# 18 instead of 20 k-tiles' adaLN on TensorE, and queries and gates of four heads moved forward, in a hybrid attention layer

## Chip, core and metric

The kernel runs on one core of a Trainium2 chip. The metric is the device time of one execution in microseconds (us), here the median of three runs. Engines are named as in the profile: TensorE (PE, with its weight loads PEld), VectorE (DVE), ScalarE (ACT), GpSimd (POOL) and SyncE (SP), whose queue issues most transfers.

## What is computed

One layer with 256 latent tokens and 256 context tokens of width 4096, all in float32. `mod` is the adaLN: a vector times a 4096 x 12288 matrix, once for `c` and (two thirds of it) once for `c_ctx`.

```python
mod = silu(c) @ ada_w + ada_b                    # shift, scale, gate: 4096 each
mod_c = silu(c_ctx) @ ada_w[:, :2*D] + ada_b[:2*D]
h  = rms_norm(x, norm_w)   * (1 + scale)   + shift
hc = rms_norm(ctx, norm_w) * (1 + scale_c) + shift_c
proj = h @ w_in                                  # queries, keys, values, gates of both groups
pc   = hc @ w_ctx                                # keys and values of the context
...                                              # A: 8 heads of differential attention; B: 8 heads of retention
y = concat([o_d * silu(dg), o_r * silu(rg)]) @ w_out
out = x + gate * y
```

## The kernel before

**Tiling.** The 4096 input features are 32 k-tiles of 128. `hs[kt]` holds k-tile kt of `h` and `hc`, transposed, for all 512 tokens, as a hi and a lo part; it exists only when the k-tile's shift and scale are known and `modulate` (L274) has applied them. Every weight tile is loaded in float32 and split too: ACT casts the hi part (L386), VectorE subtracts for the lo part (L387), and three matmuls (hi·hi, hi·lo, lo·hi) make a product (L400 to L402). A *unit* is two k-tiles of one head. A key/value unit ("kv") multiplies four row tiles (latent and context), 24 matmuls of 512 columns for a head of group A and of 384 for group B. A query/gate unit ("qg") needs the latent tokens alone: two row tiles, 12 matmuls. `run_units` (L435) prepares the weights of the next unit (`prep`, L373: three raw buffers, four hi and four lo buffers of one k-tile each), runs a unit and calls a function between units, which appends other work.

**Opening part** (to about 492 us). The first `K1` = 20 k-tiles have their adaLN on TensorE: `Ada.unit` (L240) multiplies eight k-tiles of `ada_w` by a padded `c` (matmuls `pa`, L254), and `finish` (L262) brings a chunk of two output k-tiles to the partitions with short matmuls against `sel` (L270). Between these run the kv units of heads A0 to A5 for the k-tiles that are ready (`SUnit`, L523); the sums of A0 to A4 lie in SBUF and VectorE adds to them (L559).

**First parts** (492 to 954 us). The heads in `FIRST` (A6, A7, B0 to B7) run their kv units over the first 20 k-tiles. Each head's partial sums are copied by ACT and stored to DRAM (`store_part`, L589). Meanwhile VectorE computes the adaLN of the other 12 k-tiles, in chunks of four: `ada2_task` (L296) is a generator; one step takes a slice of `ada_w` (two transfers of 256 KB) and does two accumulations (L318, L320), one for `c` and one for `c_ctx`. After 32 slices TensorE sums the accumulators over the partitions, one column at a time (L328), and `modulate` makes four more `hs`. `between1` (L607) deals the 99 steps out evenly over the first 90 of 100 units.

**Rest** (954 to about 2172 us), in the order of `SCHED`: per head, "kv" over the last 12 k-tiles, whose stored part is loaded four units before the end (L484) and added by VectorE (L495); then "qg" over all 32 k-tiles. Attention or retention of the head before runs in steps between the units (`between`, L969), and so does the gate's share of the adaLN (`gate_task`, L910), two steps a unit in "kv" of group A, one in group B, none in "qg". **Output projection**: from about 2172 us to the end.

The tile framework makes the instruction order of each engine from the order of the program and its own timing estimate, so an instruction whose inputs are ready can move ahead of its place in the program. The right-hand pool `a4` has 41 slots, which `hs`, the heads' tiles and the accumulators share.

Of the kernel before, what the change touches and what calls it, by code (L numbers as in the profile page):

```python
# [20 lines left out]
KT = D // P  # L21
# [17 lines left out]
K1 = 20  # L39
CHUNKS = [1, 1] + [2] * 9  # L40
CHUNKS2 = [4, 4, 4]
# [41 lines left out]
def hybrid_kernel(es, tc, x, c, ctx, c_ctx, norm_w, ada_w, ada_b, w_in, q_norm_w, k_norm_w,  # L83
# [21 lines left out]
    for k in "AB":  # L105
        for h in range(8):
            for i in range(2):
                p_dram[f"{k}{h}", i] = dram.tile([P, 2, 512 if k == "A" else 384], F32, name=f"p_dram{k}{h}_{i}")
# [187 lines left out]
    def ada2_task():  # L296

        work = [(j, k) for j in range(len(CHUNKS2)) for k in range(KT)]
        ahead = []

        def load():
            if len(ahead) < len(work):
                j, k = work[len(ahead)]
                ahead.append(ada_load(c0s2[j], CHUNKS2[j], k, f"ada2_{j}_{k}")[0])

# [3 lines left out]
        for i, (j, k) in enumerate(work):  # L309
            w = ahead[i]  # L310
            cn = CHUNKS2[j]
            n = cn * P
            if k == 0:
                acc = [a4.tile([P, 2 * n], F32, name=f"acc{j}_{v}", tag="a4") for v in range(2)]
            for v in range(2):
                cv = cT[:, v, k:k + 1]
                if k == 0:
                    nc.vector.tensor_scalar(acc[v], w, cv, None, op0=ALU.mult)  # L318
                else:
                    nc.vector.scalar_tensor_tensor(acc[v], w, cv, acc[v], op0=ALU.mult, op1=ALU.add)  # L320
            load()
            if k == KT - 1:
# [154 lines left out]
    def head_units(hd, qg, ktseq, part=False, rest=False):  # L477
# [6 lines left out]
        def before():  # L484
            for i in range(2):
                hd.dst(2 * i, 0)
                nc.sync.dma_start(hd.t[i], p_dram[hd.name, i])

        def after():
# [8 lines left out]
            if part:  # L498
                store_part(hd)
# [89 lines left out]
    def store_part(hd):  # L589

        for i in range(2):
            nc.scalar.dma_start(p_dram[hd.name, i], hd.t[i])
            hd.t[i] = None
# [9 lines left out]
    n_units = len(FIRST) * K1 // 2  # L603
    n_steps = len(CHUNKS2) * (KT + 1)
    done = [0, 0]

    def between1(i):  # L607
        done[0] += 1
        while done[1] < n_steps and done[1] < done[0] / (n_units - 10) * n_steps:
            next(ada2, None)  # L610
            done[1] += 1

    for nm in FIRST:
        run_units(head_units(heads[nm], 0, pairs(0, K1), part=True), between1)
# [363 lines left out]
    for item in SCHED:  # L978
# [9 lines left out]
        if kind == "qg":  # L988
            run_units(head_units(hd, 1, pairs(0, KT)), between)
# [100 lines left out]
```

## Time and profile before

| what | value |
|---|---|
| median of 3 runs | 2545.53 us (2541.44 to 2547.76) |
| the profiled execution | 2544.53 us, span of its instructions 2542.7 us |
| mean granted TensorE clock | 0.991 |
| busy: TensorE, its weight loads, VectorE, ACT | 99%, 84%, 68%, 39% |
| moved over the span | 563.70 MB, mean 222 GB/s |

Busy shares are averages over parts with different limits. The busy time of TensorE is modelled, so the pitch at which its units follow each other says more. The granted clock is the share of 2.4 GHz that TensorE was given; 0.50 is 1.2 GHz.

### The profile page before, as it was taken

What the parts mean: (1) busy time and instruction counts of PE and PEld (TensorE: products, weight loads), DVE (VectorE), ACT (ScalarE), POOL (GpSimd) and SP (SyncE); (2) the same over time, 40 slices, a digit from 0 to 9 for tenths busy, and PEclk for the clock granted to TensorE, in tenths of its full rate; (3) what the DMA queues carried; (4) which work ended last, traced back from release to release, by engine and by line L of the source; (5) the groups of instructions that cost most, each with busy time, mean ns of one, the idle gap of its engine ahead of it and who ended that gap; (6) DMA issues with size and microseconds to landing.
All of it is one profiled execution on the core that took longest, in us unless ns stands there. A gap on an engine that the chain in (4) does not pass through costs nothing.

```text
span 2542.7 us, 36389 instructions
## 1 busy us (share of the span) xinstructions
PE 2508.3 (99%) x12634; PEld 2123.9 (84%) x12634; DVE 1726.4 (68%) x3026; ACT 992.2 (39%) x2017; POOL 44.6 (2%) x47
## 2 busy tenths in 40 slices
PE   7999999999999999999999999999999999999999
PEld 4566666888999997788888788899999999878887
DVE  5555555795897946777876887777777666655554
ACT  4222222222323233354445444554444444544443
POOL 0000000000000000000000000000000000000000
PEclk8999999999999999999999999999999999999999
DMA  9987978785686748766776676556666556676765
GB/s 315 291 284 243 292 230 292 244 269 176 198 274 192 252 105 278 235 219 196 239 241 202 201 238 227 185 178 199 198 207 203 169 152 189 197 238 207 229 208 175
DMA packets 497240, 563.70 MB, mean 222 GB/s; under 512 B 31696, under 2 KB 385296, under 8 KB 497056
## 3 DMA queue, kind: packets, MB, share of 16 engines
q1 hardware_dynamic: 480336, 526.57, 65.7%
q10 hardware_dynamic: 16720, 34.81, 4.0%
q8 instruction: 99, 1.62, 0.3%
q14 instruction: 85, 0.70, 0.1%
HBM read 538.17 MB, written 23.09 MB: 221 GB/s over the span
## 4 chain that ended last, share of the span: by engine, by line
PE 91%; DMA 5%; DVE 2%; SPq 1%; issue 1%; ACT 0%; DVEq 0%; ACTq 0%
PE psA L401 7%; PE psA L402 7%; PE psA L400 7%; PE psB L401 6%; PE psB L402 6%; PE psB L400 6%; PE psO L400 5%; PE psO L401 5%; PE psO L402 5%; PE pa L254 3%; DMA graw<-in_ada_w_dram 2%; DMA ada<-in_ada_w_dram 1%; DMA ostg<-o_dram 1%; SPq L219 1%; PE psA2s L551 1%; PE psA3s L551 1%
## 5 line engine op out<-in xcount | busy, mean ns | idle before, releaser
L386 ACT CAST whiB<-rawB 128x384 fp32r<-128x384 f32 x512 | 258.8, 512 | 455.5 <-PE psB L402 176.9
L387 DVE TENSOR_TENSOR wloB<-rawB,whiB 128x384 fp32r<-128x384 f32 x512 | 279.4, 553 | 170.7 <-ACT whiB L386 166.5
L386 ACT CAST whiA<-rawA 128x512 fp32r<-128x512 f32 x392 | 241.2, 620 | 380.9 <-PE psA L402 251.5
L401 PE MATMUL psA<-wloA,h 128*128 128x512 f32 x896 | 357.8, 399 | 2.6 <-DVE wloA L387 2.5
L402 PE MATMUL psA<-whiA,h 128*128 128x512 f32 x896 | 355.5, 397 | 0.0
L387 DVE TENSOR_TENSOR wloA<-rawA,whiA 128x512 fp32r<-128x512 f32 x392 | 268.3, 687 | 113.2 <-ACT whiA L386 112.3
L400 PE MATMUL psA<-whiA,h 128*128 128x512 f32 x896 | 319.2, 398 | 0.2 <-ACT whiA L386 0.2
L401 PE MATMUL psB<-wloB,h 128*128 128x384 f32 x896 | 303.4, 339 | 1.4 <-DVE wloB L387 1.3
L402 PE MATMUL psB<-whiB,h 128*128 128x384 f32 x896 | 301.7, 337 | 0.0
L387 DVE TENSOR_TENSOR wloO<-rawO,whiO 128x512 fp32r<-128x512 f32 x256 | 175.1, 691 | 154.9 <-ACT whiO L386 154.4
L400 PE MATMUL psB<-whiB,h 128*128 128x384 f32 x896 | 263.4, 339 | 1.9 <-ACT whiB L386 1.8
L386 ACT CAST whiO<-rawO 128x512 fp32r<-128x512 f32 x256 | 157.1, 620 | 198.1 <-PE psO L402 161.5
L320 DVE SCALAR_TENSOR_TENSOR acc<-ada,cT,acc 128x1024 f32<-128x1024 f32 x186 | 233.7, 1277 | 0.0
L934 DVE SCALAR_TENSOR_TENSOR gacc<-graw,cT,gacc 128x512 f32<-128x512 f32 x248 | 184.8, 745 | 49.1 <-DMA graw<-in_ada_w_dram 47.1
L401 PEld LDWEIGHTS psA<-wloA,h 128*128 128x128 f32 x896 | 168.7, 188 | 43.6 <-DVE wloA L387 5.1
L401 PE MATMUL psO<-wloO,o 128*128 128x512 f32 x512 | 203.2, 397 | 0.0
L402 PE MATMUL psO<-whiO,o 128*128 128x512 f32 x512 | 202.8, 396 | 0.0
L400 PEld LDWEIGHTS psA<-whiA,h 128*128 128x128 f32 x896 | 168.5, 189 | 40.0 <-ACT whiA L386 0.5
L402 PEld LDWEIGHTS psA<-whiA,h 128*128 128x128 f32 x896 | 168.7, 188 | 38.9
L401 PEld LDWEIGHTS psB<-wloB,h 128*128 128x128 f32 x896 | 168.5, 188 | 4.1 <-DVE wloB L387 3.6
L402 PEld LDWEIGHTS psB<-whiB,h 128*128 128x128 f32 x896 | 168.5, 188 | 0.3
L400 PEld LDWEIGHTS psB<-whiB,h 128*128 128x128 f32 x896 | 163.0, 188 | 3.9 <-ACT whiB L386 3.2
(395 smaller groups left out, 4250.4 us busy)
## 6 DMA issues: line engine op xcount, KB each, us to landing
ada<-in_ada_w_dram SPq DMA_DIRECT2D x512, 256.0 KB, 4.7
rawA<-in_w_in_dram SPq DMA_DIRECT2D x392, 256.0 KB, 3.4
rawB<-in_w_in_dram SPq DMA_DIRECT2D x256, 256.0 KB, 3.1
graw<-in_ada_w_dram SPq DMA_DIRECT2D x128, 512.0 KB, 5.0
rawO<-in_w_out_dram SPq DMA_DIRECT2D x128, 512.0 KB, 4.5
rawB<-in_w_in_dram SPq DMA_DIRECT2D x256, 128.0 KB, 2.8
p_dramA<-kvqgA ACTq DMA_DIRECT2D x16, 512.0 KB, 2.8
kvqgA<-p_dramA SPq DMA_DIRECT2D x16, 512.0 KB, 6.7
```

What stands on the lines that cost most here:

```text
L219: nc.sync.dma_start(t[:, :, s], ada_w[k0 * P:(k0 + m) * P, s * D + c0 * P:s * D + c0 * P + n] .rearrange("(k p) n -> p k n", p=P))
L254: m = nc.tensor.matmul(self.pa[32 * g:32 * (g + 1), :], cpad[:, 2 * kt:2 * kt + 32], tiles[k], start=(u0 == 0 and i < 4), stop=(u0 + nk == ...
L320: nc.vector.scalar_tensor_tensor(acc[v], w, cv, acc[v], op0=ALU.mult, op1=ALU.add)
L386: nc.scalar.copy(hi, raw[:, k])
L387: nc.vector.tensor_tensor(lo, raw[:, k], hi.bitcast(F32), op=ALU.subtract)
L400: nc.tensor.matmul(pt[:, :ncol], a, hi, start=f, stop=False)
L401: nc.tensor.matmul(pt[:, :ncol], a, lo, start=False, stop=False)
L402: nc.tensor.matmul(pt[:, :ncol], b, hi, start=False, stop=e)
L551: nc.tensor.matmul(pt, a, hi, start=f, stop=False)
L934: nc.vector.scalar_tensor_tensor(acc, raw[:, k], cT[:, 0, kt:kt + 1], acc, op0=ALU.mult, op1=ALU.add)
```

## The change

`K1` becomes 18: the opening part has ten chunks instead of eleven (two single k-tiles, then pairs), and VectorE gets 14 k-tiles, a chunk of two and three of four. A step for the chunk of two takes two k-slices of 256 columns each for shift and scale (four accumulations of 512 columns). The qg units of A0 to A3 over the first 18 k-tiles join the first parts, after B7: their part is stored, and their "qg" in the rest covers 14 k-tiles and adds the part (`NQ` = 4). `between1` no longer counts units: each unit has a weight (`room`: 4.2 us for a kv unit of A, 3.0 for one of B, 1.4 for a qg unit), and the 116 steps are dealt out in proportion, to be through at 0.96 of the total.

```diff
--- before.py
+++ after.py
@@ -36,9 +36,11 @@
 
 
 
-K1 = 20
-CHUNKS = [1, 1] + [2] * 9
-CHUNKS2 = [4, 4, 4]
+K1 = 18
+CHUNKS = [1, 1] + [2] * 8
+CHUNKS2 = [2, 4, 4, 4]
+
+NQ = 4
 LEAD = 0.3
 NS = 6
 ADAB = 6
@@ -104,7 +106,7 @@
     p_dram = {}
     for k in "AB":
         for h in range(8):
-            for i in range(2):
+            for i in range(3):
                 p_dram[f"{k}{h}", i] = dram.tile([P, 2, 512 if k == "A" else 384], F32, name=f"p_dram{k}{h}_{i}")
 
     def aux_tile(shape, name):
@@ -295,31 +297,31 @@
 
     def ada2_task():
 
-        work = [(j, k) for j in range(len(CHUNKS2)) for k in range(KT)]
+        work = [(j, k) for j, cn in enumerate(CHUNKS2) for k in range(0, KT, 4 // cn)]
         ahead = []
 
         def load():
             if len(ahead) < len(work):
                 j, k = work[len(ahead)]
-                ahead.append(ada_load(c0s2[j], CHUNKS2[j], k, f"ada2_{j}_{k}")[0])
+                ahead.append(ada_load(c0s2[j], CHUNKS2[j], k, f"ada2_{j}_{k}"))
 
         for _ in range(ADAB - 1):
             load()
         yield
-        for i, (j, k) in enumerate(work):
-            w = ahead[i]
+        for i, (j, k0) in enumerate(work):
             cn = CHUNKS2[j]
             n = cn * P
-            if k == 0:
+            if k0 == 0:
                 acc = [a4.tile([P, 2 * n], F32, name=f"acc{j}_{v}", tag="a4") for v in range(2)]
-            for v in range(2):
-                cv = cT[:, v, k:k + 1]
-                if k == 0:
-                    nc.vector.tensor_scalar(acc[v], w, cv, None, op0=ALU.mult)
-                else:
-                    nc.vector.scalar_tensor_tensor(acc[v], w, cv, acc[v], op0=ALU.mult, op1=ALU.add)
+            for q, w in enumerate(ahead[i]):
+                for v in range(2):
+                    cv = cT[:, v, k0 + q:k0 + q + 1]
+                    if k0 + q == 0:
+                        nc.vector.tensor_scalar(acc[v], w, cv, None, op0=ALU.mult)
+                    else:
+                        nc.vector.scalar_tensor_tensor(acc[v], w, cv, acc[v], op0=ALU.mult, op1=ALU.add)
             load()
-            if k == KT - 1:
+            if k0 + 4 // cn == KT:
                 yield
                 pm = aux_tile([P, cn, 4], f"pm2_{j}")
                 for q in range(cn):
@@ -482,8 +484,8 @@
         bank = Bank(f"ps{hd.name}{'p' if part else ''}_{qg}", nrt)
 
         def before():
-            for i in range(2):
-                hd.dst(2 * i, 0)
+            for i in (2,) if qg else (0, 1):
+                hd.dst(2 * i, qg)
                 nc.sync.dma_start(hd.t[i], p_dram[hd.name, i])
 
         def after():
@@ -496,7 +498,7 @@
                 else:
                     evict(d, bank.t[rt][:, :hd.ncol])
             if part:
-                store_part(hd)
+                store_part(hd, qg)
 
         for i, (kt0, nk) in enumerate(ktseq):
             last = i == len(ktseq) - 1
@@ -586,9 +588,9 @@
     for h in range(HB):
         heads[f"B{h}"] = Head("B", h)
 
-    def store_part(hd):
-
-        for i in range(2):
+    def store_part(hd, qg=0):
+
+        for i in (2,) if qg else (0, 1):
             nc.scalar.dma_start(p_dram[hd.name, i], hd.t[i])
             hd.t[i] = None
 
@@ -600,18 +602,24 @@
 
     ada2 = ada2_task()
     next(ada2)
-    n_units = len(FIRST) * K1 // 2
-    n_steps = len(CHUNKS2) * (KT + 1)
-    done = [0, 0]
-
-    def between1(i):
-        done[0] += 1
-        while done[1] < n_steps and done[1] < done[0] / (n_units - 10) * n_steps:
+    firsts = [(nm, 0) for nm in FIRST] + [(f"A{h}", 1) for h in range(NQ)]
+    n_steps = sum(KT * cn // 4 + 1 for cn in CHUNKS2)
+
+
+    def room(nm, qg):
+        return (1.4 if qg else 4.2) if nm[0] == "A" else 3.0
+
+    total = sum(room(*f) for f in firsts) * (K1 // 2)
+    done = [0.0, 0]
+
+    def between1(i, us):
+        done[0] += us
+        while done[1] < n_steps and done[1] < done[0] / (0.96 * total) * n_steps:
             next(ada2, None)
             done[1] += 1
 
-    for nm in FIRST:
-        run_units(head_units(heads[nm], 0, pairs(0, K1), part=True), between1)
+    for nm, qg in firsts:
+        run_units(head_units(heads[nm], qg, pairs(0, K1), part=True), lambda i, us=room(nm, qg): between1(i, us))
     for _ in ada2:
         pass
     ada_cm.__exit__(None, None, None)
@@ -986,7 +994,8 @@
         hd = heads[nm]
         gate_rate[0] = 0 if kind == "qg" else 2 if hd.kind == "A" else 1
         if kind == "qg":
-            run_units(head_units(hd, 1, pairs(0, KT)), between)
+            early = hd.kind == "A" and hd.h < NQ
+            run_units(head_units(hd, 1, pairs(K1 if early else 0, KT), rest=early), between)
         else:
             run_units(head_units(hd, 0, pairs(K1, KT), rest=True), between)
         if kind == "qg":
```

## Rows read from the trace of the kernel before

**Rows 1.** By tile: duration min/median/max in ns, first and last start in us.
```profile
L400 PE MATMUL psA6p<-whiA,h x80: 392/397/400, 492.5 to 548.0; 128*128 128x512 f32 x80
...
L400 PE MATMUL psA7p<-whiA,h x80: 392/397/400, 548.7 to 604.3; 128*128 128x512 f32 x80
...
L400 PE MATMUL psB1p<-whiB,h x80: 336/336/667, 650.4 to 694.4; 128*128 128x384 f32 x80
...
L400 PE MATMUL psB2p<-whiB,h x80: 336/336/336, 694.9 to 734.9; 128*128 128x384 f32 x80
...
L400 PE MATMUL psB3p<-whiB,h x80: 336/336/336, 736.5 to 777.8; 128*128 128x384 f32 x80
...
L400 PE MATMUL psB4p<-whiB,h x80: 336/336/522, 781.6 to 823.3; 128*128 128x384 f32 x80
...
L400 PE MATMUL psB5p<-whiB,h x80: 336/336/337, 824.8 to 864.9; 128*128 128x384 f32 x80
```

**Rows 2.** Busy us in stretches: PE, PEld, DVE, ACT, POOL, then PEclk, DMA, GB/s.
```profile
606.00:648.00 42.00, 42.00 (x249) 42.00 (x248) 11.48 (x21) 12.30 (x25) 0.00 (x0) 1.00 0.40 120
...
690.00:732.00 42.00, 42.00 (x245) 42.00 (x244) 40.37 (x46) 11.90 (x24) 0.00 (x0) 1.00 0.84 272
...
970.00:1000.00 30.00, 29.92 (x128) 23.79 (x127) 25.26 (x38) 10.58 (x30) 0.00 (x0) 1.00 0.92 314
```

**Rows 3.** Chain of waits: `sel` blocks in the opening part, first and last of seven.
```profile
186.25 0.79 PE pm L270 x8
...
449.60 0.79 PE pm L270 x8
```

**Rows 4.** TensorE's groups by line, opening part, 186 to 449.5 us.
```profile
L254 PE MATMUL pa<-ada,cpad 128*32 128x512 f32 x384 | 51.1, 599 | 0.9 <-DMA ada<-in_ada_w_dram 0.9
...
L270 PE MATMUL pm<-tab,ms 128*128 128x2 f32 x50 | 6.0, 239 | 0.0
```

**Rows 5.** Chain of waits: two of the three column sums of VectorE's adaLN.
```profile
646.73 3.84 PE pm L328 x32
...
778.48 3.24 PE pm L328 x30
```

**Rows 6.** Stretches of 5 us behind a `sel` block and behind column sums.
```profile
183.00:188.00 5.00, 5.00 (x31) 3.50 (x29) 3.74 (x8) 1.24 (x2) 0.00 (x0) 1.00 0.66 222
...
650.00:655.00 5.00, 5.00 (x17) 5.00 (x18) 3.87 (x10) 2.16 (x5) 0.00 (x0) 0.50 0.20 58
```

**Rows 7.** Timeline of VectorE beside A7: start, us, what.
```profile
574.06 1.28 DVE L320 SCALAR_TENSOR_TENSOR acc<-ada,cT,acc 128x1024 f32<-128x1024 f32 x1
575.26 0.68 DVE L387 TENSOR_TENSOR wloA<-rawA,whiA 128x512 fp32r<-128x512 f32 x1
575.86 1.28 DVE L320 SCALAR_TENSOR_TENSOR acc<-ada,cT,acc 128x1024 f32<-128x1024 f32 x1
577.69 0.69 DVE L387 TENSOR_TENSOR wloA<-rawA,whiA 128x512 fp32r<-128x512 f32 x1 [0.55 <-ACT whiA L386]
...
595.17 2.47 DVE L320 SCALAR_TENSOR_TENSOR acc<-ada,cT,acc 128x1024 f32<-128x1024 f32 x2
```

**Rows 8.** The page's costliest groups: the gate's accumulation.
```profile
L934 DVE SCALAR_TENSOR_TENSOR gacc<-graw,cT,gacc 128x512 f32<-128x512 f32 x248 | 184.8, 745 | 49.1 <-DMA graw<-in_ada_w_dram 47.1
```

**Rows 9.** VectorE's accumulations by line, beside A6 and A7, and beside B2.
```profile
L320 DVE SCALAR_TENSOR_TENSOR acc<-ada,cT,acc 128x1024 f32<-128x1024 f32 x62 | 77.3, 1278 | 0.0
...
L320 DVE SCALAR_TENSOR_TENSOR acc<-ada,cT,acc 128x1024 f32<-128x1024 f32 x26 | 32.8, 1278 | 0.0
```

**Rows 10.** The page's DMA issues: adaLN slices.
```profile
ada<-in_ada_w_dram SPq DMA_DIRECT2D x512, 256.0 KB, 4.7
```

**Rows 11.** Waits of SP's queue: total us, times, longest.
```profile
SPq L219 <- DVE acc L320: 88.1, 77, 2.8
```

**Rows 12.** Group A in the rest: TensorE by tile, and one stretch.
```profile
L402 PE MATMUL psA<-whiA,h x896: 388/397/481, 956.2 to 1647.8; 128*128 128x512 f32 x180
...
1200.00:1300.00 100.00, 100.00 (x460) 81.47 (x459) 75.33 (x146) 48.07 (x110) 5.08 (x5) 1.00 0.67 210
```

## Prediction

> **What bounds the kernel now.** I read the page's slices of the span first. They show TensorE near full nearly everywhere, but that share is modelled, so it only says where to look. The better test is the pitch of the work. In the first parts (from 492 us) a kv head of group A takes 548.7 − 492.5 = 56.2 us for 10 units and B2 takes 736.5 − 694.9 = 41.6 us for 10 [rows 1]: 5.62 and 4.16 us a unit, 24 matmuls each, so 234 ns per 512 columns and 173 ns per 384. The granted clock there is 1.00 and VectorE is up to 96% busy (40.37 of 42 us) with no effect on that pitch [rows 2]. From 492 us to the end the bound is TensorE's own work, at full clock but for the dips priced below. The one place where TensorE does much that is not a projection is the opening part, where its k-tiles' adaLN runs between projection units. Its blocks of sel matmuls come 43.9 us apart on the chain of waits ((449.60 − 186.25)/6) [rows 3], and six units of 5.62 us are only 33.7 of that.
>
> **What the change removes.** One chunk of two k-tiles leaves the opening part. Its six projection units are not saved: they return in the "rest" units, as do the units that the first parts lose. Units over all: opening −6 of A; first parts −2 of A and −8 of B; rest +8 of A and +8 of B. That is zero for each kind. The 36 query/gate units of A0 to A3 only change place, also zero. What goes is the period less its units, 43.9 − 33.7 = **−10.2 us**. The grouped rows give the lower bound: adaLN matmuls 51.1 us over six chunks and sel matmuls 6.0 us, 9.5 a chunk [rows 4]. The difference is short waits inside the period, and I take them as going with it.
>
> **What it adds on TensorE.** The two k-tiles come back as column sums of VectorE's accumulators (L328). A chunk of four takes 32 matmul instructions, 3.84 us on the chain for the first chunk (for the second 30 instructions and 3.24 us) [rows 5]; a chunk of two has half of them: **+1.75 us**. Behind such a block the granted clock falls, behind the first from 650 to 655 us to 0.50, the 1.2 GHz level, though TensorE counts as busy all through the block; behind an eight-instruction block of the opening part it stays at 1.00 [rows 6]. The price is read from the next head: B1 takes 694.9 − 650.4 = 44.5 us, 2.9 over 41.6, and B4 824.8 − 781.6 = 43.2, 1.6 over [rows 1]. For a block of 16 the ends are 0 and 2.9; it lies between the two sorts, so **+0.9**.
>
> The Trainium skill, "TensorE: Matmul & The Clock Gate", section "HAM oscillation — how this bites in real kernels", has the clock fall behind gaps in which TensorE idles. Here it falls behind matmuls of one column with no idle gap. By that rule nothing is added and the sum is 0.9 lower; the row decides.
>
> **What it adds on VectorE, and its cover.** Starts in the timeline give true spacing: a 1024-column accumulation holds VectorE 1.20 us, a lo split 0.60 [rows 7]; the 512-column form has a mean of 745 ns in the gate's sums, 0.66 after the same overlap [rows 8]. So the new chunk costs 64 × 0.66 = 42 us, each chunk of four 64 × 1.20 = 77, and the modulate four 256-column instructions per k-tile, 14 × 4 × 0.39 = 22 us (0.39 is an estimate, the line through 0.66 and 1.20 carried on to 256 columns): 295 us. All lies behind TensorE in the first parts, which grow from 10 heads × 10 units (445 us) to 18 × 5.62 + 72 × 4.16 + 36 × 2.81 = 502 us. Measured capacity: VectorE does 62 accumulations beside A6 and A7 and is through with the chunk at 597.6 us, 105 us or 18.7 units after the start, so 3.3 a unit; a B unit takes 2.6 (26 in 10) [rows 7, 9]. A query/gate unit leaves 2.81 − 1.20 = 1.6 us, 1.3 accumulations.
>
> Is each accumulator ready when TensorE comes to its column sums? The new dealing orders 116 steps over 0.96 × 342 us, so the sums stand behind unit 11 of A, unit 22 of B, unit 53 of B and query/gate unit 25. Chunk 1 needs 42/4.2 = 10 units and has 11. Chunk 2: 7 × 3.3 + 22 × 2.6 = 80, less 3 for the modulate with its waits for ACT, against 64. Chunk 3: 31 × 2.6 − 7 = 73 against 64. Chunk 4: 19 × 2.6 − 7 = 42 before the query/gate units, and the last 22 need 17 of the 25. All are met, by 5 to 22 us. Before, VectorE stood idle after the first chunk was summed (11.48 of 42 us busy in B0 [rows 2]); that slack is what is spent.
>
> **Transfers.** A query/gate unit loads 512 KB in 2.81 us, and 0.65 of an adaLN step's 512 KB (two transfers of 256 KB [rows 10]) makes 308 GB/s, with the part stores more. TensorE ran unhindered at 272 GB/s with the DMA engines at 0.84 (690 to 732 us), and for 30 us at 314 with 0.92 [rows 2]. So the queues are nearly full for some 17 units. Bounds: nothing, or what R3 and R4 below charge; I take **+2 us**, two late weight tiles. SP takes these issues in order, and its waits for an accumulation to free a slot were 1.14 us each (88.1 in 77) [rows 11]; raw weights queue behind them.
>
> The Trainium skill, "DMA: Bandwidth & Descriptors" (its opening table), gives a core some 358 GB/s of HBM. By it the 308 fits and the 2 us fall away; the highest stretch among the rows is 314.
>
> **Later stages.** Parts of queries and gates are stored and loaded again: 4 stores of 512 KB on ACT's queue, 4 loads on SP's, each issued four units (11 us) before its add, and a part copy by ACT and two adds by VectorE in place of one copy each. Heads A0 to A3 then have 14 units instead of 22 to hide 17 attention steps. A head takes (1647.8 − 956.2)/8 = 86.5 us now with VectorE at 75% [rows 12], 65 us. It will take 86.5 − 9 × 2.81 + 5.62 = 67 us, and VectorE's work falls by 16 lo splits and grows by 4 gate accumulations, to some 57 us, 85%. The density inside a kv unit is as before (one step, two gate steps), so I charge nothing; without that cover it is one step of 1.2 us in each of 28 units, 34 us. Gate steps move forward (112 instead of 96 in group A), which frees VectorE in group B, where it limits nothing.
>
> **Sum.** −10.2 + 1.75 + 0.9 + 2 = −5.5 us. The profiled execution took 2544.5 us, so 2539.0. The median of the runs shown is 1.0 higher: **2540.0**. What can be told from no change is 0.3%, 7.6 us either way.
>
> **Rivals.**
>
> R1 (forecast, 0.44): as above, 2536 to 2543. One seventh of it lies below 2537.9.
>
> R2, nothing hinders and the clock holds (0.24): −10.2 + 1.75 = −8.4, so 2537. For it: full rate in B2 with VectorE at 96%. Against: no unit of 2.81 us has yet had accumulations beside it.
>
> R3, VectorE sets the pace of the query/gate units (0.19): the other side. An adaLN step cannot be split, and only four hi/lo buffers cover it: two k-tiles ahead, 2.81 us in these units. A unit that takes a step needs 2 × 0.60 + 2 × 1.20 and the 0.55 us for which VectorE waits for ACT before a lo split [rows 7], 4.15 us; 1.34 too much. At 12.5 steps in 25 units it is 17 us. Without the 2 us, which it replaces, the sum is −7.5: −7.5 + 17 = +9.5, 2555. It decides for slower from 15 us on, 0.6 us in each of 25 units. Against it: beside A7 VectorE alternated splits and accumulations almost without a gap [rows 7] and TensorE lost nothing.
>
> R4, TensorE waits at the last column sums (0.13): if transfers hold at the 272 GB/s of B2, a query/gate unit has 272 × 2.81 = 764 KB, less 524 for its weights and 58 for stores, 182 KB or 0.7 accumulations. By unit 25 some 17 of the last 22 are done; TensorE waits for 5 × 1.20 = 6 us and runs on at the lower clock, 2.9 more: −7.5 + 8.9 = +1.4, 2547. It begins at 280 GB/s and below (0.88 a unit); the 314 of one stretch speaks against. Here also belongs that the dealing does nothing: VectorE already ran accumulations ahead of their place in the program (idle in B0, the first column sums at 646.7 [rows 2, 5]), so the order moves only TensorE's column sums.
>
> **Chances.** Faster: R2 and a seventh of R1, 0.30. Slower: R3, 0.19. Same: the rest, 0.51. The range 2534 to 2553 holds R1, R2 and R4, and leaves out R3; R1's own is 2536 to 2543.
>
> **What would show it.** Right: ten sel blocks instead of eleven, first parts beginning near 448 us; four L328 blocks, the first of 16 instructions and 1.7 us in A7; B heads of 37.4 us for nine units; the four query/gate parts 25.3 us each; clock dips behind three or four blocks. R3 shows as query/gate parts of 28 us and more with PE released by a lo split; R4 as one gap ahead of the last L328 block released by L320. The prediction is wrong if A0 to A3 take over 72 us a head, or if SP's issues of raw weights stand behind a wait for a slot of the right-hand pool.

## The result and the profile after

The changed kernel takes 2587.84 us (median of 4 runs, 2583.83 to 2592.04), the kernel before on the same chip 2544.57: ratio 1.0173, 95% interval 1.0155 to 1.0192. It is slower by 1.7% where no change was forecast. The profiled execution took 2586.11 us.

The page of after: its span, two engines, the slices, the chain, and two groups (busy us, mean ns, idle time ahead of them and what ended it).

```profile
span 2584.3 us, 36320 instructions
PE 2513.1 (97%) x12578; PEld 2128.6 (82%) x12578; DVE 1754.1 (68%) x3074; ACT 986.5 (38%) x2020; POOL 45.7 (2%) x47
...
PE   7999999999999999999899989999999999999999
...
PE 37%; DMA 6%; DVE 5%; issue 1%; ACT 0%; SPq 0%; POOL 0%; DVEq 0%; ACTq 0%; POOLq 0%
...
L403 PE MATMUL psA<-wloA,h 128*128 128x512 f32 x816 | 330.2, 405 | 10.9 <-DVE wloA L389 10.9
...
L942 DVE SCALAR_TENSOR_TENSOR gacc<-graw,cT,gacc 128x512 f32<-128x512 f32 x248 | 185.3, 747 | 85.1 <-DMA graw<-in_ada_w_dram 82.8
```

Two things differ from before. The slices of TensorE now have two dips (the 8s, 1228 to 1292 and 1486 to 1551 us). And the chain, which was 91% TensorE, can be followed back only to 1308 us, into group A's stage, where it runs over landings of the gate's loads (4% of the span) and its sums (2%); most of its 37% of TensorE lies later, in group B's stage and the output. The gate's accumulation takes the same time as in [rows 8] (747 ns), but VectorE stands idle ahead of it for 85.1 us, not 49.1.

Which stage lost is read from first starts by tile.

```profile
L402 PE MATMUL psA6p<-whiA,h x72: 391/397/401, 450.1 to 500.0; 128*128 128x512 f32 x72
...
L402 PE MATMUL psB4p<-whiB,h x72: 335/336/337, 708.0 to 745.0; 128*128 128x384 f32 x72
...
L402 PE MATMUL psB5p<-whiB,h x72: 335/337/668, 745.5 to 789.1; 128*128 128x384 f32 x72
...
L402 PE MATMUL psA0p<-whiA,h x36: 391/396/461, 864.5 to 890.3; 128*128 128x512 f32 x36
...
L402 PE MATMUL psA3p<-whiA,h x36: 391/397/401, 946.7 to 970.9; 128*128 128x512 f32 x36
```

The first parts begin at 450.1 us instead of 492.5 [rows 1], and B4 has its pitch (37.5 us for nine units). A stage's time "by its units" in the table is that of the kernel before plus the units that come and less those that go, at 5.62, 4.16 and 2.81 us (2.08 for a qg unit of B); the loss is what is measured above it. Each stage time is read from one profiled execution: the unchanged opening part takes 444.3 to 451.6 us in the traces of the kernels with 18 k-tiles, so a few us in one stage say nothing.

| stage | before | after | difference | by the prediction's terms | over |
|---|---|---|---|---|---|
| opening part | 492.5 | 450.1 | −42.4 | −43.9 | +1.5 |
| first parts | 462.6 | 525.7 | +63.1 | 56.7 + 1.75 + 0.9 + 2 = +61.4 | +1.7 |
| rest, group A | 692.9 | 674.6 | −18.3 | 8 × 5.62 − 36 × 2.81 = −56.2 | **+37.9** |
| rest, group B | 522.7 | 561.3 | +38.6 | 8 × 4.16 = +33.3 | +5.3 |
| output | 372.0 | 372.6 | +0.6 | 0 | +0.6 |
| span | 2542.7 | 2584.3 | +41.6 | −5.4 | +47.0 |

The loss is in group A's stage. Stretches of it (busy us of PE, PEld, DVE, ACT, POOL, then clock, DMA share, GB/s):

```profile
1000.00:1100.00 100.00, 100.00 (x438) 80.54 (x437) 82.39 (x147) 41.03 (x90) 2.55 (x1) 1.00 0.78 257
1100.00:1200.00 100.00, 98.84 (x455) 80.13 (x454) 78.04 (x147) 38.74 (x90) 3.75 (x3) 1.00 0.75 241
1200.00:1300.00 100.00, 89.83 (x403) 72.14 (x402) 73.50 (x143) 36.26 (x86) 4.20 (x4) 0.95 0.62 197
...
1400.00:1500.00 100.00, 91.23 (x407) 72.75 (x406) 74.40 (x143) 40.71 (x93) 4.60 (x3) 0.97 0.67 209
```

VectorE is not the fuller where TensorE loses: it has 82 us of work from 1000 to 1100, with TensorE full, and 73.5 from 1200 to 1300, less than before [rows 12], with TensorE at 89.8. So TensorE loses its time in waits, beside a VectorE that has time left. Over the whole stage (the same columns, before and after) TensorE is idle 2.6 and 30.4 us:

```profile
955.10:1648.00 692.90, 690.29 (x3114) 558.24 (x3115) 526.97 (x991) 316.93 (x695) 26.98 (x21) 1.00 0.70 223
```

```profile
975.80:1650.40 674.60, 644.16 (x2845) 516.26 (x2846) 510.29 (x970) 275.17 (x627) 26.32 (x19) 0.98 0.69 222
```

That is 27.8 of the 37.9 us. The rest, some 10 us, is work at the lower clock, to which TensorE falls behind several of these waits (the last section has a row). Behind what TensorE waits (total us, times, longest):

```profile
PE psA L403 <- DVE wloA L389: 10.9, 9, 2.0
PE aTpA L139 <- DVE pA L790: 10.1, 4, 5.5
PE psA L402 <- ACT whiA L388: 7.5, 4, 5.8
PE poA L720 <- DVE aTA L714: 1.8, 1, 1.8
```

So 12 us end with the attention's own steps, and 18 with the lo and hi parts of weights that come late. How the first sort comes about is in the timelines of VectorE, ACT, TensorE and SP's queue (start, us, what, idle time before it and what ended it):

```profile
1264.31 1.54 DVE L942 SCALAR_TENSOR_TENSOR gacc<-graw,cT,gacc 128x512 f32<-128x512 f32 x2 [2.04 <-DMA graw<-in_ada_w_dram]
...
1271.02 0.69 DVE L780 TENSOR_REDUCE stA<-scA 128x1 f32<-128x512 f32 x1 [2.19 <-PE scA L720]
1273.49 0.75 DVE L942 SCALAR_TENSOR_TENSOR gacc<-graw,cT,gacc 128x512 f32<-128x512 f32 x1 [1.78 <-DMA graw<-in_ada_w_dram]
1274.16 0.68 DVE L780 TENSOR_REDUCE stA<-scA 128x1 f32<-128x512 f32 x1
...
1279.29 0.75 DVE L942 SCALAR_TENSOR_TENSOR gacc<-graw,cT,gacc 128x512 f32<-128x512 f32 x1 [0.82 <-DMA graw<-in_ada_w_dram]
1279.96 0.75 DVE L790 SCALAR_TENSOR_TENSOR pA<-pA,stA,pA 128x512 f32<-128x512 f32 x1
```

```profile
1274.94 0.78 ACT L783 ACTIVATE pA<-scA,stA,qsA 128x512 f32<-128x512 f32 x1 [9.30 <-DVE stA L781]
...
1277.20 0.45 PE L139 MATMUL aTpA<-tab,pA 128*128 128x128 f32 x1 [5.53 <-DVE pA L790]
1280.76 0.90 PE L139 MATMUL aTpA<-tab,pA 128*128 128x128 f32 x3 [3.12 <-DVE pA L790]
1282.59 1.65 PE L402 MATMUL psA<-whiA,h 128*128 128x512 f32 x3 [0.93 <-ACT whiA L388]
```

```profile
1260.85 0.88 SPq L380 DMA_DIRECT2D rawA<-in_w_in_dram  x2
1262.30 0.37 SPq L923 DMA_DIRECT2D graw<-in_ada_w_dram  x1
1265.88 1.57 SPq L489 DMA_DIRECT2D kvqgA<-p_dramA  x2
1268.86 12.90 SPq L923 DMA_DIRECT2D graw<-in_ada_w_dram  x3
1283.97 5.83 SPq L380 DMA_DIRECT2D rawA<-in_w_in_dram  x4
```

Read the four together. A gate sum (L942) stands in VectorE's order between the two score reductions (L780); its load has not landed, so VectorE waits 1.78 us with the second reduction ready behind it. ACT, which takes the exponential next, has then been idle for 9.30 us; the second weighted sum (L790) follows another gate sum and another wait of 0.82; and TensorE, whose order has the attention's transposes (L139) next, stands 5.53 and 3.12 us. Of these 8.65 us some 4.6 are the gate's: waits of 1.78 and 0.82 and three sums of 0.67. On SP's queue the raw weights wait behind the gate's issues.

The longest of TensorE's waits is of the other sort. ACT has the cast of a finished gate sum (`gah`) in its order ahead of the weights' casts, and it is idle 7.47 us until VectorE, which waits for landings here too, has summed:

```profile
1494.96 0.62 ACT L713 CAST gah<-gacc 128x512 fp32r<-128x512 f32 x1 [7.47 <-DVE gacc L942]
1495.48 1.65 ACT L388 CAST whiA<-rawA 128x512 fp32r<-128x512 f32 x3
```

```profile
1496.15 1.22 PE L402 MATMUL psA<-whiA,h 128*128 128x512 f32 x2 [5.76 <-ACT whiA L388]
```

The first case is in a kv unit of A4, and the softmax is that of A2. In the kernel before the heads came 86.5 us apart and so did their attention; a head's softmax fell behind the next head's kv part, beside qg units, which have no gate steps. In after the kv parts of A0 to A3 end 62 to 68 us apart (1018.6, 1080.6, 1149.1, 1213.2), but the attention follows at 93 on average: the ropes of A0 and of A4 start 371 us apart.

```profile
L705 DVE TENSOR_TENSOR t1A0k<-kvqgA,tab x4: 273/274/274, 1050.5 to 1051.1; 128x128 f32<-128x128 f32 x4
...
L705 DVE TENSOR_TENSOR t1A4k<-kvqgA,tab x4: 278/280/280, 1421.7 to 1422.3; 128x128 f32<-128x128 f32 x4
```

In before A4's rope (1399.7) stands ahead of the adds that end A5's kv part (1422); in after it stands behind them (1394). And it is behind A3's kv part that time is lost: those of A4 to A7 end 80.6, 102.9, 100.1 and 104.2 us after the one before. The first of these stretches holds A3's short qg and should take 67 us, the others, with 16 qg units, 86.5 + 5.62 = 92.1: some 45 us over, of which the stretches of A1 to A3 had gained 6.

### The profile page after: what moved, and what is told of

Read it like the earlier page. It is cut to its first block, busy times and chain, and to the rows that moved or that the text cites. A ratio compares the mean times of both kernels' runs of the same rounds, so it can differ in the third digit from the quotient of the medians.

```text
span 2584.3 us, 36320 instructions
## 1 busy us (share of the span) xinstructions
PE 2513.1 (97%) x12578; PEld 2128.6 (82%) x12578; DVE 1754.1 (68%) x3074; ACT 986.5 (38%) x2020; POOL 45.7 (2%) x47
## 5 line engine op out<-in xcount | busy, mean ns | idle before, releaser
L388 ACT CAST whiA<-rawA 128x512 fp32r<-128x512 f32 x404 | 246.9, 619 | 395.4 <-PE psA L404 192.9
L403 PE MATMUL psA<-wloA,h 128*128 128x512 f32 x816 | 330.2, 405 | 10.9 <-DVE wloA L389 10.9
L403 PE MATMUL psB<-wloB,h 128*128 128x384 f32 x960 | 325.8, 339 | 3.5 <-DVE wloB L389 3.3
L404 PE MATMUL psA<-whiA,h 128*128 128x512 f32 x816 | 326.4, 400 | 0.0
L404 PE MATMUL psB<-whiB,h 128*128 128x384 f32 x960 | 323.7, 337 | 0.0
L402 PE MATMUL psA<-whiA,h 128*128 128x512 f32 x816 | 289.0, 404 | 10.8 <-ACT whiA L388 10.8
L402 PE MATMUL psB<-whiB,h 128*128 128x384 f32 x960 | 285.9, 339 | 3.6 <-ACT whiB L388 3.6
L322 DVE SCALAR_TENSOR_TENSOR acc<-ada,cT,acc 128x1024 f32<-128x1024 f32 (+1 forms) x248 | 276.9, 1144 | 0.0
L942 DVE SCALAR_TENSOR_TENSOR gacc<-graw,cT,gacc 128x512 f32<-128x512 f32 x248 | 185.3, 747 | 85.1 <-DMA graw<-in_ada_w_dram 82.8
L403 PEld LDWEIGHTS psA<-wloA,h 128*128 128x128 f32 x816 | 155.7, 191 | 52.1 <-DVE wloA L389 16.1
L402 PEld LDWEIGHTS psA<-whiA,h 128*128 128x128 f32 x816 | 154.9, 191 | 48.1 <-ACT whiA L388 12.9
L403 PEld LDWEIGHTS psB<-wloB,h 128*128 128x128 f32 x960 | 180.9, 188 | 6.5 <-DVE wloB L389 5.9
L404 PEld LDWEIGHTS psA<-whiA,h 128*128 128x128 f32 x816 | 156.0, 191 | 35.1
L404 PEld LDWEIGHTS psB<-whiB,h 128*128 128x128 f32 x960 | 180.9, 188 | 0.1
L402 PEld LDWEIGHTS psB<-whiB,h 128*128 128x128 f32 x960 | 175.7, 188 | 5.5 <-ACT whiB L388 4.9
```

The lines of the kernel that those rows point to most:

```text
L388: nc.scalar.copy(hi, raw[:, k])
L402: nc.tensor.matmul(pt[:, :ncol], a, hi, start=f, stop=False)
L403: nc.tensor.matmul(pt[:, :ncol], a, lo, start=False, stop=False)
L404: nc.tensor.matmul(pt[:, :ncol], b, hi, start=False, stop=e)
L942: nc.vector.scalar_tensor_tensor(acc, raw[:, k], cT[:, 0, kt:kt + 1], acc, op0=ALU.mult, op1=ALU.add)
```

## The experiments

Three theories. **V**: VectorE's extra adaLN, 14 k-tiles instead of 12, costs. **P**: the attention's own pace of some 85 to 90 us a head, which shorter heads of A no longer cover. **G**: the gate's steps; group A's stage has 112 of them instead of 96 (two a kv unit) in 56 us less, and VectorE, which takes its work in order, waits for each landing with attention behind it. Where a kernel's loss in group A's stage is told, it is its time over that by its units.

**Which part of the change.** `e1_move_only` keeps 20 k-tiles and only moves A0 to A3's queries and gates; `e2_group_B` moves those of B0 to B4 instead of A0 to A3; `e3_no_move` moves none.

```diff
# e1
-K1 = 18; CHUNKS = [1, 1] + [2] * 8; CHUNKS2 = [2, 4, 4, 4]
+K1 = 20; CHUNKS = [1, 1] + [2] * 9; CHUNKS2 = [4, 4, 4]
# e2
-    firsts = [(nm, 0) for nm in FIRST] + [(f"A{h}", 1) for h in range(NQ)]
+    firsts = [(nm, 0) for nm in FIRST] + [(f"B{h}", 1) for h in range(5)]
-            early = hd.kind == "A" and hd.h < NQ
+            early = hd.kind == "B" and hd.h < 5
# e3
-NQ = 4
+NQ = 0
```

> The kernel before (20 k-tiles' adaLN on TensorE) with only the queries and gates of A0 to A3 moved into the first parts. Theory P (pace): the attention of a group-A head is a serial chain of 85 to 100 us and the heads' chains follow one another, so shortening a head's projections to 61 us gains nothing in the A part; expected: A part some 30 to 45 us longer than its units (591 us by units: 692.9 less 101.2), total 2575 to 2590. Theory G (gate): the gate's steps have become denser and VectorE and ACT wait for their loads; 12 steps in 61 us a head is as dense as in the changed kernel, so also 2575 or more. Theory V (VectorE's two further k-tiles cost the time): no loss, 2540 to 2550.

> The changed kernel, but the queries and gates that join the first parts are those of B0 to B4 (weight 1.1 us a unit) and A0 to A3 keep theirs in the rest. P: the A part follows the attention's pace again, 692.9 + 45 = 738 us without loss, and what the B part can't hide of retention is small; total 2535 to 2550. G: a head of group A has 14 gate steps in 92 us, about the density of before, so also near 2540. V: slow as the changed kernel, 2575 or more.

> The changed kernel with no query/gate units moved (18 k-tiles on TensorE, 14 on VectorE in first parts of 90 units). P: A part 738 us without loss; the first parts have some 292 us of VectorE's time for 295 us of work and lose 5 to 20 us; total 2540 to 2560. G: as P. V: 2575 or more.

| | time, us | ratio (95%) | group A's stage, by its units | loss there |
|---|---|---|---|---|
| after | 2587.84 | 1.0173 (1.0155 to 1.0192) | 674.6, 636.7 | 37.9 |
| e1_move_only | 2606.17 | 1.0244 (1.0226 to 1.0262) | 626.8, 580.5 | 46.3 |
| e2_group_B | 2558.78 | 1.0062 (1.0045 to 1.0079) | 742.0, 737.9 | 4.1 |
| e3_no_move | 2554.59 | 1.0045 (1.0029 to 1.0060) | 754.0, 737.9 | 16.1 |

With 20 k-tiles 40 units are moved, so e1's stage is 692.9 − 40 × 2.81 = 580.5 by its units. The move alone costs more than the whole change: V falls. With the same adaLN as in after and group A's heads left whole, e2's stage loses 4 us; its other loss is 15 us in the first parts (529.6 against 514.4 by units with the new column sums), whose cause was not looked for. The number of gate steps in the stage does not rank these: e1 has 96, as before, and loses 46; e2 has 112, as in after, and loses 4. Most of e3's 16 us lie at the stage's beginning, behind the last column sums. TensorE stands 7.45 us there for the hi parts of its first weights, and ACT takes their casts behind the issues of small tables (L636 to L695), while transfers run at 324 GB/s:

```profile
880.00:900.00 20.00, 12.39 (x41) 9.57 (x42) 10.12 (x18) 4.46 (x10) 0.00 (x0) 0.74 0.94 324
...
892.45 0.33 ACTq L695 DMA_DIRECT2D wq_b<-in_diff_q_norm_w_dram  x1
892.82 2.18 ACT L388 CAST whiA<-rawA 128x512 fp32r<-128x512 f32 x4 [11.16 <-DMA subln<-in_diff_subln_w_dram]
```

In after the moved units stand between the column sums and this place, where TensorE waits 3.25 us.

**P or G.** `e4_gate_later` takes gate steps out of group A, one a kv unit, and puts two into B's; `e5_gate_fitted` has one in A0 to A3 alone; `e10_spread` keeps two and moves the queries and gates of A0, A2, A4 and A6, so that no two short heads follow each other.

```diff
# e4
-        gate_rate[0] = 0 if kind == "qg" else 2 if hd.kind == "A" else 1
+        gate_rate[0] = 0 if kind == "qg" else 1 if hd.kind == "A" else 2
# e5
+        gate_rate[0] = 0 if kind == "qg" else 2 if hd.kind == "A" and hd.h >= NQ else 1
# e10
+EARLY = ['A0', 'A2', 'A4', 'A6']
-            early = hd.kind == "A" and hd.h < NQ
+            early = nm in EARLY
```

> The changed kernel with the gate's steps dealt one a unit in group A's key/value units and two in group B's, instead of two and one. P: the A part stays near 675 us and the heads' outputs stay 85 to 100 us apart; total 2575 to 2592. G: half as many gate steps in group A, the waits for their loads go and the A part falls to 640 to 650 us; total 2545 to 2560, unless group B then waits for the gate.

> The changed kernel with one gate step a unit in the key/value units of A0 to A3, whose heads have become shorter, two in A4 to A7 as before, one in group B. If the density of the gate's steps in the short heads is the cause, the A part takes 637 to 645 us instead of 674.6 and the B part 556 to 561, total 2540 to 2548, near or just below the kernel before. If the attention's pace is the cause, the A part stays at 665 or more, total 2575 or more.

> The changed kernel, with A0, A2, A4 and A6 in place of A0 to A3 as the heads whose queries and gates move. By units the A part is the same 636.7 us. If the attention and the gate's sums fall behind in a short head and catch up in a long one, the A part takes 640 to 660, total 2550 to 2570. If each short head costs its 9 us wherever it stands, 670 to 680, total 2580 or more.

e4: 2558.70 us, 1.0049 (1.0032 to 1.0067); group A's stage 635.3, no loss. e5: 2560.12, 1.0064 (1.0050 to 1.0078); 644.7, loss 8.0. e10: 2560.31, 1.0072 (1.0048 to 1.0095); 652.4, loss 15.7. So with as many units, gate steps and short heads as in after, 22 of the 37.9 us go when no two short heads follow each other. The same stretch of e4:

```profile
1200.00:1300.00 100.00, 98.63 (x448) 79.52 (x447) 69.82 (x145) 48.03 (x121) 6.24 (x4) 1.00 0.55 169
1300.00:1400.00 100.00, 100.00 (x457) 80.77 (x456) 71.77 (x142) 46.18 (x102) 3.66 (x3) 1.00 0.60 187
1400.00:1500.00 100.00, 100.00 (x457) 81.30 (x456) 68.07 (x133) 48.43 (x108) 3.98 (x3) 1.00 0.56 182
```

TensorE is full, though the heads are as short as in after and the attention still lags (A0's and A4's ropes 334 us apart, 83 a head). So a late attention alone does not stop TensorE: P falls for group A's stage, and the gate's steps are needed for the loss. e5 says which: it leaves those beside A4 to A7 as they are and thins only those beside A0 to A3, and 30 of the 37.9 us, which are lost behind A3's kv part, go. What e4 wins there it gives back in part: group B's stage is 570.8 against 556 by units.

**Which side of a gate step.** `e6_half_sums` does one of a step's two accumulations; `e7_half_loads` loads half and does both on it; `e8_gate_own_queue` issues the loads from GpSimd, so that SP's order has no part in them; `e9_gate_ahead` loads two steps ahead instead of one.

```diff
# e6
-            for k in range(2):
+            for k in range(1):
# e7
-                nc.sync.dma_start(raw, ada_w[u * 2 * P:(u + 1) * 2 * P, ...
+                nc.sync.dma_start(raw[:, 0], ada_w[u * 2 * P:u * 2 * P + P, ...
# e8
-            with tc.issue_after(last_raw[0]):
-                nc.sync.dma_start(raw, ...
+                nc.gpsimd.dma_start(raw, ...
# e9
-        nxt = load(0)
+        nxt = [load(0), load(1)]
-            raw = nxt
-            if v + 1 < n:
-                nxt = load(v + 1)
+            raw = nxt.pop(0)
+            if v + 2 < n:
+                nxt.append(load(v + 2))
```

> The changed kernel with one of the two accumulations of each gate step left out (the gate lacks its odd k-tiles); all loads stay. If VectorE's time is what the gate's steps take too much of, the A part falls to 637 to 650 us, total 2545 to 2560. If it is their loads (their landing, and weights queued behind them on SP), it stays at 660 to 675, total 2570 to 2588.

> The changed kernel with half of each gate step's load left out: 256 KB in place of 512, and both accumulations read the same half (the gate is computed from wrong rows). If the gate's loads are the cause, the A part falls to 637 to 650 us, total 2545 to 2560. If it is VectorE's time, it stays at 660 to 675, total 2570 to 2588.

> The changed kernel with the gate's loads issued by GpSimd instead of SyncE, so that no raw weights stand behind them. If SP's order is the cause (a gate load that waits for its slot holds the weights back), the A part falls to 637 to 655 us, total 2545 to 2565. If VectorE's in-order wait for the landing or VectorE's time is the cause, the A part stays at 660 or more, total 2570 or more.

> The changed kernel with the gate's loads issued two steps ahead instead of one. If VectorE's in-order wait for a gate load's landing is what delays the attention behind it, the waits (82.8 us) shrink and the A part falls from 674.6 to 645 to 660 us, total 2553 to 2570. If the sums' own time or the slots of the right-hand pool are the cause, it stays at 668 or more, total 2578 or more.

| | time, us | ratio (95%) | group A's stage | loss there |
|---|---|---|---|---|
| e6_half_sums | 2550.66 | 1.0031 (1.0019 to 1.0043) | 649.5 | 12.8 |
| e7_half_loads | 2558.49 | 1.0058 (1.0035 to 1.0081) | 648.9 | 12.2 |
| e8_gate_own_queue | 2596.01 | 1.0205 (1.0180 to 1.0231) | 674.3 | 37.6 |
| e9_gate_ahead | 2565.56 | 1.0092 (1.0068 to 1.0116) | 662.4 | 25.7 |

Both halves of a gate step matter, its sums and its landing; SP's order is not needed for the loss: off SP's queue it is 37.6. GpSimd's queue waits too, above all for the gate's own sums to free a slot. Waits of e8's queue (total us, times, longest), then the gate's group in e9:

```profile
POOL graw L923 <- DVE gacc L942: 328.9, 67, 25.5
```

```profile
L942 DVE SCALAR_TENSOR_TENSOR gacc<-graw,cT,gacc 128x512 f32<-128x512 f32 x248 | 185.6, 748 | 58.1 <-DMA graw<-in_ada_w_dram 56.1
```

**What is left, and a control.** `e13_ahead_half_sums` joins e9 and e6; `e15_fitted_ahead` e9 and e5; `e16_before_ahead` is the kernel before with e9's edit alone.

> The gate's loads two steps ahead as in e9, and one of each step's two accumulations left out as in e6 (the gate's odd k-tiles are missing from the output). Two steps ahead left group A's stage at 662 us against 637 by its units. Theory S (what is left there is VectorE's time for the sums, since the landings are now covered): about 640 us in that stage, 2540 in all. Theory W (what is left is still waits for landings or the number of transfers): 655 us or more, 2553 and up.

> After with one gate step a unit in A0 to A3 (as in e5) and the gate's loads two steps ahead. e5 lost 8 us in group A's stage and 8 in group B's over its units. Theory G (both are landings that VectorE waits for in its order, with attention behind): most of the 16 come back, 2540 to 2546 us. Theory P (attention that lags behind its heads is what reaches into group B): no more than 5 come back, 2553 to 2558.

> The kernel before with the gate's loads two steps ahead, nothing else. There TensorE is at its units' time in both stages, the waits for landings lie behind it. Theory G: same within 0.2%, 2540 to 2547. Rival (the 47.1 us that VectorE waits for landings there cost time already, so that e9's gain is no part of what the change brought): 2525 to 2537.

e13: 2544.04 us, 1.0006 (0.9997 to 1.0015); group A's stage 641.5, loss 4.8. So of the 37.9 us the earlier loads take 12, halving the sums 21 more. e15: 2552.43, 1.0037 (1.0025 to 1.0050); the stage at 636.9, no loss, but group B's at 565.8 against 556: the 8 us of e5 in group A were landings, those in group B were not, and what they are stays open; its time is the number of neither theory. e16: 2540.40, 0.9987 (0.9978 to 0.9995). The control matters: by the ratios e9's edit gains (1.0173 − 1.0092) × 2543 = 21 us in after and 0.0013 × 2543 = 3 in before, so some 17 of the 21 undo what the change brought. Only part of it is in the stage in question: by the traces that is 12.2 us shorter in after and 2.2 in before, and of the rest 5.8 are in the opening part, which the edit does not touch.

The total of VectorE's waits is no measure of the loss. In e5 it waits longer for the gate's loads than in after, and loses 8 us where after loses 38:

```profile
L942 DVE SCALAR_TENSOR_TENSOR gacc<-graw,cT,gacc 128x512 f32<-128x512 f32 x248 | 185.7, 749 | 98.8 <-DMA graw<-in_ada_w_dram 97.0
```

**Where a gate step stands.** The loss in after shows behind A3's kv part, not in A0 to A3 themselves, where gate steps are densest. Theory **M**: it comes where the late softmax meets gate steps. Theory **D**: it is their number or density. `e17_gate_beside_qg` moves the steps of A4 to A7 beside qg units; `e18_before_gate_qg` does so in the kernel before for all of group A.

```diff
# e17
-        gate_rate[0] = 0 if kind == "qg" else 2 if hd.kind == "A" else 1
+        late = hd.kind == "A" and hd.h >= NQ
+        gate_rate[0] = (1 if late else 0) if kind == "qg" else 0 if late else 2 if hd.kind == "A" else 1
# e18
+        gate_rate[0] = (1 if kind == "qg" else 0) if hd.kind == "A" else 0 if kind == "qg" else 1
-        for _ in range(gate_rate[0]):
+        for _ in range(gate_rate[0] if i < 12 else 0):
```

> After with group A's gate steps of A4 to A7 moved from their kv units (two a unit) to their query/gate units (one a unit, 64 steps instead of 56); A0 to A3 keep two a kv unit, so group A's stage holds no fewer gate steps than in after. In after the kv parts of A4 to A7 end 80.6, 102.9, 100.1 and 104.2 us apart, and the softmax of the attention two heads back falls into them (1257, 1349, 1439, 1534 us), where in the kernel before it falls behind them, beside units without gate steps. Theory M (the loss comes where the late softmax meets the gate's steps): group A's stage goes from 675 to 637 to 650 us, 2548 to 2562 in all. Theory D (it is the number of gate steps in the stage, or their density in A0 to A3): the stage stays over 665 us, 2577 and more.

> The kernel before with group A's gate steps beside its softmax: instead of two in each of a head's six kv units, one in each of the first 12 of its 16 query/gate units, so the same 12 a head in the same 34 us, only moved against the attention. Theory M: group A's stage of 693 us grows by 5 to 15 us a head that meets its softmax, 2570 to 2640 in all. Theory D: same number, same density, 2540 to 2550.

e17: 2583.10 us, 1.0150 (1.0126 to 1.0175); group A's stage 670.9, loss 34.2. M's number does not come. e18: 2575.70, 1.0123 (1.0102 to 1.0144); the stage 719.7 against 692.9, loss 26.8, with the same number of steps at the same density in time: D's number does not come either. One stretch of e17 and one of e18:

```profile
1200.00:1300.00 100.00, 99.57 (x450) 80.17 (x449) 72.90 (x140) 41.88 (x95) 3.67 (x3) 1.00 0.62 196
...
1400.00:1500.00 100.00, 84.12 (x370) 66.07 (x368) 71.08 (x139) 41.98 (x112) 4.82 (x4) 0.91 0.63 200
```

```profile
1100.00:1200.00 100.00, 96.36 (x433) 76.75 (x433) 73.79 (x143) 44.53 (x99) 3.75 (x3) 1.00 0.67 216
...
L934 DVE SCALAR_TENSOR_TENSOR gacc<-graw,cT,gacc 128x512 f32<-128x512 f32 x248 | 185.4, 748 | 113.5 <-DMA graw<-in_ada_w_dram 112.9
```

In e17 the loss of 1200 to 1300 is gone, and a larger one stands at 1400. e18 shows why that cannot decide: beside a qg unit a gate step costs in itself, since two lo splits and two sums are 2 × 0.60 + 2 × 0.66 = 2.5 of its 2.81 us [rows 7, 8], and what TensorE waits for in e18's stage is the lo split, not the softmax:

```profile
PE psA L401 <- DVE wloA L387: 18.0, 21, 2.0
```

So the place of a gate step against the other work is worth 27 us by itself. Number alone is out, by e1 and e2. M alone is doubtful: in e5 the softmax of A3 and of A4 still falls into kv units with two gate steps (1331 to 1348 us for A3's, where A5's kv part ends at 1371), and 8 us are lost. What fits the runs of the changed kernel is gate steps that come too densely in short heads one after the other (e4, e5, e10); how their price is carried over to A4 to A7 was not settled.

**Toward a faster version.** `e11_two_heads` moves A0 and A1 alone, with one gate step a unit there; `e12_free_heads` moves A0, B5 and B6; `e14_free_heads_ahead` is e12 with loads two ahead.

```diff
# e11
+EARLY = ['A0', 'A1']
+        gate_rate[0] = 0 if kind == "qg" else 2 if hd.kind == "A" and hd.h >= 2 else 1
# e12
+EARLY = ['A0', 'B5', 'B6']
```

> The changed kernel with the queries and gates of A0 and A1 alone moved, and one gate step a unit in the key/value units of these two. By units the A part is 687.3 us, the first parts 471. If the losses come from the number of short heads, A takes 687 to 693 and the first parts 473 to 485, total 2537 to 2550.

> The changed kernel with the queries and gates of A0 (beside which no attention runs yet), B5 and B6 (beside which VectorE is 55 to 65% busy) moved. By units the A part is 712.6 us, the first parts 483. If only attention and gate sums beside the short head make it dear, A takes 713 to 718, the B part 515 to 525, total 2537 to 2550, the lowest of the versions with 18 k-tiles; if the attention's pace sets A and B as before, no difference to the two-head version.

> The three heads whose kv units no longer meet a denser gate (A0, B5, B6 moved, as in e12) with the gate's loads two steps ahead. By its units the span is 2534. Theory G (landings of the gate's loads cost what e12 lost): 2536 to 2539 us. Rival (e12's 5 us over its units are in the first parts, at the dense transfers of its moved units, where no gate runs): no change against e12, 2542 to 2545.

e11: 2541.55 us, 1.0003 (0.9989 to 1.0018), loss in group A 6.4. e12: 2543.46, 1.0001 (0.9991 to 1.0011), loss in group A 2.2. e14: 2539.80, 0.9989 (0.9980 to 0.9998); its trace, of the slowest of 11 runs, shows e12's rest in group A at no loss (713.4 against 712.6), and 7 us lost in the first parts (490.1 against 483.4). No version beats the kernel before by more than 0.1%; e16's one edit, without the change, gives as much.

## Why the prediction was wrong

**The step that failed** is the one on the later stages: "The density inside a kv unit is as before (one step, two gate steps), so I charge nothing". It costs 37.9 us. A density inside a unit is not the one that counts: a short head has 14 gate steps in 67 us, where a head had 12 in 86.5. The working beside it had the reason in hand: 14 units for 17 attention steps, heads of 67 us instead of 86.5. It compared VectorE's work with the time (57 of 67 us) and took what fits for hidden. But VectorE and ACT take their work in order and part of it waits for loads (the two timelines); what they have in capacity they do not have in order. e4 shows that without the dense gate steps the stage runs at its units' time, e9 and e13 that landings and sums both pay. The working also had no term for the clock behind such waits, some 10 of the 37.9 us.

**The bound was there and left out.** "without that cover it is one step of 1.2 us in each of 28 units, 34 us" is near the 37.9 by its size, though its mechanism (work too much for VectorE in A0 to A3) is not what the trace shows; that the sizes agree is luck. A bound of 34 us belongs in the range or to a rival.

**The signs that were named for it.** A0 to A3 were to take over 72 us a head; they took 62 to 68, and the time is lost behind them, mostly in heads that the change hardly touches. Raw weights behind a wait for a slot on SP's queue are there (the gate's issues of 1268.86 last 12.90 us), but SP's queue waits as long for the gate's sums in before (77.8 us in group A's stage against 73.6), and e8 loses the same without them.

**What held.** The opening part: −42.4 us for a period of 43.9. The first parts: +63.1 for 61.4, so column sums, clock and late weights together came out 1.7 us above 4.65. The parts of that did not all hold: the block of 16 makes A7 1.8 us longer and brings no clock dip, where +0.9 was charged; dips came behind two blocks, not three or four. Ahead of group A's stage the kernel stands 3.2 us from the forecast.

**The rivals.** R3 priced VectorE as the bound of the four query/gate parts at 28 us each; from 864.5 to 975.8 us they took 111.3, less 3.84 of column sums 26.9 each, against 25.3, 6 us over. That is not R3: 3.25 of the 6 are the wait for group A's first weights at their end, and waits that end at a lo split are 1.0 us in all. R4's wait at the last column sums is not seen in after; its limit of 280 GB/s should be 289 by its own terms (0.88 of 262 KB, 524 and 58 in 2.81 us). R2, in which nothing hinders, was right on the opening part alone. No rival had the place where the time went.

## What to carry to other kernels

When units are taken out of a stage, everything that was dealt out by units (background steps, streamed loads, sums) becomes denser in time and changes its place against the rest, and the price can fall on later work that is itself unchanged. Do not test cover by busy time alone on an engine that takes its work in order: list what stands in its order ahead of the step that the bounding engine awaits, and ask whether any of it waits for a transfer. A background stream that loads one step ahead wants a second step of lookahead before its neighbours are shortened; and an engine's total of waits says little (98.8 us cost 8, 85.1 cost 38), the busy share and the granted clock of the bounding engine by stretches say where they cost.

## What the runs showed of the hardware

The clock behind column sums depends on the block. Behind the block of 16 (its last 14 from 514.5 us) it stays at the upper level. Behind the second (28 of 32 together, from 645.1) and the third (its last 30 from 779.0) it falls to 0.50, the 1.2 GHz level, as in [rows 6], with TensorE busy all the time. The fourth comes in pieces, the longest of 18, and the clock stays. (The row of [rows 6] for the `sel` block lies mostly ahead of it; the 5 us behind, 188 to 193 in before, are at 1.00 too.) Transfers go higher than any stretch of before that was read: 332 GB/s over 5 us with the DMA engines at 0.98.

```profile
516.00:520.00 4.00, 4.00 (x19) 3.28 (x19) 3.71 (x10) 1.80 (x4) 0.00 (x0) 1.00 0.14 46
...
783.00:788.00 5.00, 5.00 (x17) 5.00 (x17) 3.78 (x10) 2.28 (x5) 0.00 (x0) 0.50 0.02 7
...
794.00:799.00 5.00, 5.00 (x30) 4.96 (x29) 5.00 (x7) 2.43 (x5) 0.00 (x0) 1.00 0.98 332
...
1277.00:1285.00 8.00, 3.76 (x10) 2.61 (x11) 5.46 (x11) 3.53 (x7) 0.00 (x0) 0.50 0.42 128
```

TensorE's waits also cost clock: from 1277 to 1285 us, behind the wait of 5.53 us, it is 0.50, over 1200 to 1300 0.95 with TensorE busy 89.83 of 100 us, and 0.91 in e17 where it is busy 84.12. The Trainium skill, "TensorE: Matmul & The Clock Gate", section "HAM oscillation — how this bites in real kernels", has the clock fall behind such gaps; here, unlike behind column sums, the trace agrees. Not every wait does it: the short ones of e18 (18.0 us in 21, none over 2.0) left it at 1.00 over the whole stage.
